# Wider projections and four query blocks at a time in a hybrid streaming-encoder block

## Chip and metric

The kernel runs on one core of one Trainium2 chip. The metric is device time in microseconds of one execution, median of several runs. Everything is single precision: operands are 32-bit, and a matrix product is done as three matmuls of split operands (below).

## The reference

One layer with 1024 tokens and 1024 channels. Three token mixers share one input projection; each is projected back to 1024 channels, gated and summed; then come an output projection, a residual and a gated feed-forward part. Shortened:

```python
h = rmsnorm(x, norm_mix_g); z = h @ w_in
hq, hf, hi, hg, fq, fk, fv, ff, mq, gate_logits = split(z)
y_a = hgrn2(hq, hf, hi, hg)            # 4 heads, 128x128 state
y_b = fox(fq, fk, fv, ff)              # 8 heads of 64
y_c = memory_attention(mq, mem_kv)     # 4 heads, 256 tokens
gates = sigmoid(gate_logits)           # 3 x 1024 columns
merged = sum(gates[b] * (y_b @ w_br[b]) for b in 3 branches)
x = x + merged @ w_out
x = x + (gelu(conv3(h2 @ w_up_a)) * (h2 @ w_up_v)) @ w_down   # 2816 wide
# fox, per head and block of 128 queries:
s = q @ k.T / 8 + F[q] - F[k]          # q, k normalised per head; k <= q
o = softmax(s) @ v
```

## The kernel before

A product is `mm3` (L158 to L162): both operands are split into a rounded high part and the rest, and three matmuls (high x high, high x low, low x high) accumulate in one PSUM bank. `split` (L172) casts on ScalarE and subtracts on VectorE. Weights come through `weights` (L188): a load from SP into one of two `raw` buffers, then a split into `wh` and `wl`, three buffers of each, 1024 columns a buffer.

The program is written as generators that are interleaved by `weave` and by priorities (`ahead`, a higher priority for the attention); the scheduler then puts the instructions of each engine into one fixed order, using a simulated timeline, before anything runs. `tc.issue_after(x)` puts an instruction behind `x` on the engine's queue. On the chip each engine works through its queue in order.

The stages, by the profile: the opening, the first gates and pairs of gate chunks as 7-product block multiplications (to about 200 us); values of the forgetting attention with the memory attention (to 310); the forgetting attention (to about 665); the recurrence with the branches' projections (to about 975); the output projection (to 1062); the way up (to 1477); the way down.

The forgetting attention is what most of the change touches. Heads come in four pairs `p`. `fox_proj(p)` (L844) projects the keys and queries of a pair, 256 columns, with `token_major` (L704): for each of 8 token blocks, 8 chunks x 3 matmuls with the tokens stationary and 256 columns moving. Its `evac` scales the result into `z` and, after four blocks, normalises it per head. `fox_prep(p)` (L866) transposes `z` and builds the split operands. `fox_attn(p, i)` (L901) takes the query blocks two at a time (`tp`): logits by two matmuls (L924, L925), masked maximum, exponential, reciprocal and scaling; then for each pair of key blocks transposes (L953 to L956) into one bank, a split, and products with the values (L965, L966) over 256 query columns; at the end of each of the four groups `yp` is added up and stored.

While a head runs, TensorE gets other work from the second argument of `weave`: for the first head of pair `p` the projection of pair `p + 1`, for the second head three gate chunks (`gates_early`, two halves of 24 matmuls of 512 columns each). During the last pair it is one gate and `hgrn_values` (L1012), the recurrence's values, in two parts of 256 columns.

Further on, `branch(br, ...)` (L1280) projects one branch: 8 chunks `j` x 2 halves, each step 12 matmuls of 512 columns, with the gates loaded back from memory from SP. Before `branch(0)` all eight loads of the memory branch's outcome (`yc`, 512 KB each) are issued from POOL. In the way up, `unit` (L1452) loads its weights in two halves from POOL into one of two `rw` buffers; `families` (L1495) makes the split block operands of the tokens, two of which (`B21`, chunks 2 and 3) have their subtraction on POOL.

Of the kernel before, what the change touches and what calls it, by code (L numbers as in the profile page):

```python
# [30 lines left out]
NFOX = [0, 3, 0, 3, 0, 3, 1]  # L31
# [3 lines left out]
assert 2 + NCOVER + NPAIR + sum(NFOX) == len(ORDER) and len(_dense) % 2 == 0  # L35
# [5 lines left out]
FOX_LATE = 0.2  # L41
SEQ = ("w0 x0 s0 w1 x1 s1 w2 x2 s2 w3 x3 s3 w4 x4 s4 x5 s5 x6 s6 x7 s7 u0 u1 u2 u3 mn u4 u5 u6 u7 lk k0 k1 k2 k3 lx "
# [67 lines left out]
def tile_block(ctx: ExitStack, tc: tile.TileContext, xT, memT, x_rows, mem_rows, vec, fbias, mats, hmask, w_first, w_cm, w_hi, w_fqk, w_fv,  # L110
# [77 lines left out]
    def weights(src, shape, raw=None, hl=None, parts=1):  # L188
# [4 lines left out]
        if hl is None:  # L193
            hl = [wp.tile([P, 4 * 264], F32R, tag=t, name=t, bufs=3) for t in ("wh", "wl")]
# [227 lines left out]
    def first_weights(k):  # L422
        k0, k1 = WFIRST[k]
        if k % 4 == 0:
            gw[k // 4] = [wp.tile([P, 4 * 264], F32R, tag=t, name=t, bufs=3) for t in ("wh", "wl")]
        sl = slice((k0 % 4) * 256, (k1 - 1) % 4 * 256 + 256)
        split(S, gw[k // 4][0][:, sl], gw[k // 4][1][:, sl], wg[k // 4][:, sl])
# [131 lines left out]
    class Dense:  # L559
# [16 lines left out]
        def operand(self, src):  # L576
            if self.half is None:
                self.half = [wp.tile([P, 4 * 264], F32R, tag=t, name=t, bufs=3) for t in ("wh", "wl")]
# [264 lines left out]

    def fox_proj(p):  # L844

        fox_z[p] = [None, None]

        def evac(tb, ps):
            n, b = tb // 4, tb % 4
            if b == 0:  # L850
                fox_z[p][n] = pq.tile([P, 4, 256], F32, tag="z", name=f"z{p}_{n}", bufs=2)
            z = fox_z[p][n]
            S.activation(z[:, b, :], ps, AF.Copy, scale=rt[:, tb:tb + 1])
            if b == 3:
                zz = z.rearrange("p b (h d) -> p (b h) d", d=64)
                sq = pools["pf"].tile([P, 16, 64], F32, tag="pt", name="fsq", bufs=4) if p else \
                    pm.tile([P, 16, 64], F32, tag="fsq", name="fsq")
                r = cp.tile([P, 16], F32, tag="fr", name="fr", bufs=2)
                S.activation(sq, zz, AF.Square)
                V.reduce_sum(r, sq, axis=AX.X)  # L860
                rstd_small(r, r, 64)
                V.tensor_mul(zz, zz, r.unsqueeze(2).to_broadcast([P, 16, 64]))

        yield from token_major(w_fqk[p], 256, evac)

# [35 lines left out]
    def fox_attn(p, i):  # L901
# [8 lines left out]
        for tp in range(4):  # L910
            pts = []
            for j in range(2):
                tb = 2 * tp + j
# [26 lines left out]
                S.activation(pt[:, :ns], pt[:, :ns], AF.Exp, bias=st[:, 2:3], accum_out=st[:, 3:4])  # L940
                V.reciprocal(st[:, 3:4], st[:, 3:4])  # L941
                G.tensor_scalar(pt[:, :ns], pt[:, :ns], st[:, 3:4], 0.0, ALU.mult, ALU.add)  # L942
# [3 lines left out]
            for sp in range(tp + 1):  # L946
                ptr = ps_tr()
                w = 384 if sp == tp else 512
                for jj in range(2):
                    sb = 2 * sp + jj  # L950
                    ssl = slice(sb * P, (sb + 1) * P)
                    if sb <= 2 * tp:
                        PE.transpose(ptr[:, jj * 256:jj * 256 + P], pts[0][:, ssl], ident)  # L953
                        PE.transpose(ptr[:, jj * 256 + P:jj * 256 + 256], pts[1][:, ssl], ident)
                    else:
                        PE.transpose(ptr[:, 256:384], pts[1][:, ssl], ident)  # L956
# [858 lines left out]
```

## Time and profile before

| | |
|---|---|
| median of 3 runs | 1699.96 us (1698.77 to 1700.16) |
| profiled execution, time | 1700.23 us |
| profiled execution, span from first to last instruction | 1698.4 us |
| mean granted TensorE clock | 0.999 |
| instructions | 24291, of which 8957 matmuls |
| moved by DMA | 227.16 MB, mean 134 GB/s |

The span is shorter than the time by what lies before the first and behind the last instruction. In the rows, PE is the matmul part of TensorE, PEld its loading of stationary operands (beside the matmuls), DVE VectorE, ACT ScalarE, POOL GpSimd, SP the engine that only issues DMAs. A group's row gives busy time and mean ns of one instruction, then the idle time just before them and what ended it. A timeline's row gives start, length, engine, line, operation, output and inputs, shape and count. A row of waits reads: who waited, for whom, total us, times, longest.

### The profile page before, as it was taken

The numbers are of one execution on the slowest core, as the hardware profiler recorded it, in microseconds if no ns is written. First come the engines' busy times: TensorE is split into PE (matmuls) and PEld (weight loads), VectorE is DVE, ScalarE is ACT, GpSimd is POOL, SyncE is SP. The second block draws the span as 40 slices with busy tenths as digits, with TensorE's granted clock in tenths as the row PEclk, the third lists the DMA queues.
The fourth block names the chain that finished last, engine by engine and source line by source line (L and its number), as shares of the span: only waits on it lengthen the run. The fifth ranks groups of instructions, "written<-read, shape, count | busy, mean of one in ns | idle before, by whom it ended". The sixth has DMA issues, their size and how long they took to land.

```text
span 1698.4 us, 24291 instructions
## 1 busy us (share of the span) xinstructions
PE 1691.0 (100%) x8957; PEld 1452.4 (86%) x8957; DVE 1150.8 (68%) x2057; ACT 800.9 (47%) x1428; POOL 324.6 (19%) x420
## 2 busy tenths in 40 slices
PE   9999999999999999999999999999999999999999
PEld 7888899989898998888888888888888888888887
DVE  6966455666666664886856845987878888775654
ACT  6734455545454553775631333644434444533432
POOL 0200032543433331544310000311111111100000
PEclk9999999999999999999999999999999999999999
DMA  9443232221212111110346542566544344494772
GB/s 367 157 161 106 88 139 68 77 92 51 94 59 77 63 46 57 67 32 13 106 127 209 167 186 100 165 174 169 158 139 138 118 149 143 172 363 145 251 269 87
DMA packets 83062, 227.16 MB, mean 134 GB/s; under 512 B 9712, under 2 KB 12408, under 8 KB 82816
## 3 DMA queue, kind: packets, MB, share of 16 engines
q1 hardware_dynamic: 64320, 160.54, 26.8%
q0 software_dynamic: 18048, 64.50, 13.2%
q8 instruction: 70, 1.15, 0.3%
q10 hardware_dynamic: 576, 0.59, 0.1%
q14 instruction: 48, 0.39, 0.1%
HBM read 180.72 MB, written 67.93 MB: 146 GB/s over the span
## 4 chain that ended last, share of the span: by engine, by line
PE 99%; DVE 0%; ACT 0%; DMA 0%; issue 0%; ACTq 0%; DVEq 0%
PE pp L160 21%; PE pp L162 21%; PE pp L161 21%; PE lg L160 4%; PE lg L162 4%; PE lg L161 4%; PE tr L162 3%; PE tr L161 3%; PE tr L160 3%; PE po L966 1%; PE lg L925 1%; PE lg L924 1%; PE po L965 1%; PE po L160 1%; PE po L161 1%; PE po L162 1%
## 5 line engine op out<-in xcount | busy, mean ns | idle before, releaser
L160 PE MATMUL pp<-uh,wh 128*128 128x512 f32 x412 | 163.3, 396 | 0.0
L161 PE MATMUL pp<-ul,wh 128*128 128x512 f32 x412 | 162.9, 395 | 0.0
L162 PE MATMUL pp<-uh,wl 128*128 128x512 f32 x412 | 162.5, 394 | 0.0
L161 PE MATMUL pp<-wl,uh 128*128 128x256 f32 (+1 forms) x512 | 146.3, 286 | 0.0
L162 PE MATMUL pp<-wh,ul 128*128 128x256 f32 (+1 forms) x512 | 146.1, 286 | 0.0
L160 PE MATMUL pp<-wh,uh 128*128 128x256 f32 (+1 forms) x512 | 145.6, 286 | 0.0
L166 ACT CAST wh<-s 128x512 fp32r<-128x512 f32 x110 | 66.5, 621 | 131.6 <-PE pp L161 55.1
L166 ACT CAST wh<-raw 128x1024 fp32r<-128x1024 f32 (+2 forms) x76 | 67.6, 890 | 100.6 <-PE pp L161 86.2
L166 ACT CAST wh<-rw 128x512 fp32r<-128x512 f32 x87 | 53.2, 619 | 108.1 <-PE pp L161 70.2
L160 PEld LDWEIGHTS pp<-wh,uh 128*128 128x128 f32 x512 | 97.3, 190 | 1.2
L161 PEld LDWEIGHTS pp<-wl,uh 128*128 128x128 f32 x512 | 97.4, 190 | 1.0
L162 PEld LDWEIGHTS pp<-wh,ul 128*128 128x128 f32 x512 | 97.4, 190 | 0.9
L1457 POOL DMA_DIRECT2D rw<-in_w_up x44 | 24.1, 555 | 372.4 <-DVE wl L1350 171.3
L166 ACT CAST dwh<-wr 128x1024 fp32r<-128x1024 f32 (+1 forms) x41 | 40.2, 980 | 115.8 <-PE tr L161 40.0
L162 PEld LDWEIGHTS pp<-uh,wl 128*128 128x128 f32 x412 | 77.5, 188 | 15.1
L174 DVE TENSOR_TENSOR wl<-raw,wh 128x1024 fp32r<-128x1024 f32 (+2 forms) x75 | 78.0, 1040 | 17.8 <-ACT wh L166 17.6
L160 PEld LDWEIGHTS pp<-uh,wh 128*128 128x128 f32 x412 | 77.5, 188 | 14.6
L161 PEld LDWEIGHTS pp<-ul,wh 128*128 128x128 f32 x412 | 77.5, 188 | 14.5
L940 ACT ACTIVATE pt<-pt,st 128x128 f32<-128x128 f32 (+3 forms) x64 | 49.7, 777 | 41.7 <-DVE st L937 33.9
L174 DVE TENSOR_TENSOR dwl<-wr,dwh 128x1024 fp32r<-128x1024 f32 (+1 forms) x41 | 46.3, 1129 | 31.7 <-ACT dwh L166 31.7
L942 POOL TENSOR_SCALAR pt<-pt,st 128x128 f32<-128x128 f32 (+3 forms) x64 | 49.1, 767 | 78.4 <-DVE st L941 64.1
L1350 DVE TENSOR_TENSOR wl<-rw,wh 128x512 fp32r<-128x512 f32 x69 | 47.7, 704 | 22.7 <-PE pp L162 18.2
(500 smaller groups left out, 5123.2 us busy)
## 6 DMA issues: line engine op xcount, KB each, us to landing
rw<-in_w_up POOLq DMA_DIRECT2D x44, 512.0 KB, 4.7
sd<-in_w_dn POOLq DMA_DIRECT2D x30, 512.0 KB, 6.0
br<-yd SPq DMA_DIRECT2D x30, 512.0 KB, 5.0
raw<-in_w_cm SPq DMA_DIRECT2D x24, 512.0 KB, 3.4
gd<-gt SPq DMA_DIRECT2D x48, 256.0 KB, 2.0
gt<-gd SPq DMA_DIRECT2D x48, 256.0 KB, 2.7
yd<-fc SPq DMA_DIRECT2D x44, 256.0 KB, 2.2
wr<-sd SPq DMA_DIRECT2D x20, 512.0 KB, 4.5
```

Of the source, the lines that this page charges most:

```text
L160: PE.matmul(ps, lh, rh, start=first, stop=False, skip_group_check=more)
L161: PE.matmul(ps, lh, rl, start=False, stop=False, skip_group_check=more)
L162: return PE.matmul(ps, ll, rh, start=False, stop=last, skip_group_check=more)
L166: return S.copy(out, in_)
L174: return (sub or V).tensor_sub(l, src, h.bitcast(F32))
L924: PE.matmul(ps[:, :w], qa[i][:, tsl], kh[i][:, s0:s0 + w], start=True, stop=False)
L925: fox_sets[p][3] = PE.matmul(ps[:, :w], qa[i][:, tsl], kl[i][:, s0:s0 + w], start=False, stop=True)
L940: S.activation(pt[:, :ns], pt[:, :ns], AF.Exp, bias=st[:, 2:3], accum_out=st[:, 3:4])
L942: G.tensor_scalar(pt[:, :ns], pt[:, :ns], st[:, 3:4], 0.0, ALU.mult, ALU.add)
L965: PE.matmul(o, vhl[:, sb, :], ph[:, src], start=(sb == 0), stop=False)
L1350: late["split"] = V.tensor_sub(l, src, h.bitcast(F32))
L1457: late["raw"] = G.dma_start(raw[:, 2 * i:2 * i + 2, :], src[:, 2 * i:2 * i + 2, :])
```

## The change

- Keys and queries of pairs 2 and 3 are projected together, 512 columns (`fox_proj_late`), each token block stored to memory (`zd`); `fox_load(p)` loads a pair back and normalises it. Pair 3's load runs in the second head of pair 1.
- The recurrence's values are projected in one part of 512 columns. `token_major` takes four weight buffers of two chunks for 512 columns, and `wh` and `wl` have four buffers (`WIDE`) instead of three.
- `fox_attn` takes four query blocks at a time: transposes of four blocks into one bank, products with the values over up to 512 columns, `yp` twice a head. `pt` has one buffer for each of the eight blocks.
- The norm's square goes through two halves in gate tiles (`fox_norm`).
- The ten early gates are spread differently over the heads (`first`, `second`).
- Each of the eight `yc` loads stands behind a one-column POOL operation that reads a gate tile just loaded, in steps 1, 2, 4, 5, 7, 8, 10 and 11 of `branch(0)`.
- The second unit's weight loads of the way up stand behind the last POOL subtraction of `B21`.
- The scratch of POOL's transfers is set to 4096 bytes.

```diff
-NFOX = [0, 3, 0, 3, 0, 3, 1]
+NFOX = 10
+WIDE = 4
@@ token_major
-            w = [weights(src[q], (4, ncol)) for q in range(2)]
+            per = 2 if ncol == HB else 4
+            w = [weights(src[q], (per, ncol)) for q in range(KC // per)]
...
-                wh, wl = w[k // 4]
-                mm3(ps, uh[k][:, tsl], ul[k][:, tsl], wh[:, k % 4, :], wl[:, k % 4, :], k == 0, k == KC - 1)
+                wh, wl = w[k // per]
+                mm3(ps, uh[k][:, tsl], ul[k][:, tsl], wh[:, k % per, :], wl[:, k % per, :], k == 0, k == KC - 1)
@@ before fox_proj
+    zd = tc.dram_tile([8, P, HB], F32, name="zd")
+    def fox_norm(z):
+        zz = z.rearrange("p b (h d) -> p (b h) d", d=64)
+        r = cp.tile([P, 16], F32, tag="fr", name="fr", bufs=2)
+        for i in range(2):
+            sq = gate_tile().rearrange("p (g d) -> p g d", d=64)
+            S.activation(sq, zz[:, 8 * i:8 * i + 8, :], AF.Square)
+            V.reduce_sum(r[:, 8 * i:8 * i + 8], sq, axis=AX.X)
+        rstd_small(r, r, 64)
+        V.tensor_mul(zz, zz, r.unsqueeze(2).to_broadcast([P, 16, 64]))
...
+    def fox_proj_late():
+        def evac(tb, ps):
+            t = gate_tile()
+            S.activation(t, ps, AF.Copy, scale=rt[:, tb:tb + 1])
+            SP.dma_start(zd[tb], t)
+        yield from token_major(w_late[0], HB, evac)
+    def fox_load(p):
+        cs = slice((p - 2) * 256, (p - 1) * 256)
+        for n in range(2):
+            z = fox_tile(p, n)
+            SP.dma_start(z, zd[4 * n:4 * n + 4, :, cs].rearrange("b p c -> p b c"))
+            fox_norm(z)
+            yield
@@ fox_attn
-        for tp in range(4):
+        for g in range(2):
...
-                pt = pf.tile([P, T], F32, tag="pt", name="pt", bufs=4)
+                pt = pf.tile([P, ns], F32, tag=f"pt{tb}", name=f"pt{tb}")
...
-            for sp in range(tp + 1):
+            for sb in range(4 * g + 4):
                 ptr = ps_tr()
+                first = max(sb - 4 * g, 0)
+                for j in range(first, 4):
+                    PE.transpose(ptr[:, j * P:(j + 1) * P], pts[j][:, sb * P:(sb + 1) * P], ident)
...
+                c = slice(first * P, HB)
+                split(S, ph[:, c], pl[:, c], ptr[:, c])
+                PE.matmul(po[:, c], vhl[:, sb, :], ph[:, c], start=sb == 0, stop=False)
+                PE.matmul(po[:, c], vhl[:, sb, :], pl[:, c], start=False, stop=sb == 4 * g + 3)
@@ the order of the pairs
+    late_proj = fox_proj_late()
+    first = (fox_proj(1), chain(islice(late_proj, 4), fox_load(2)), gates_early(2))
+    second = (chain(gates_early(1), islice(late_proj, 4)), gates_early(3), gates_early(3))
     for p in range(3):
-        weave((ahead(fox_attn(p, 0), AHEAD), FOX_STEPS), (fox_proj(p + 1), 8))
+        weave((ahead(fox_attn(p, 0), AHEAD), FOX_STEPS), (first[p], (8, 6, 4)[p]))
         fox_prep(p + 1, fox_sets[p][3])
-        weave((ahead(fox_attn(p, 1), AHEAD), FOX_STEPS), (gates_early(NFOX[2 * p + 1]), 2 * NFOX[2 * p + 1], FOX_LATE))
+        weave((ahead(fox_attn(p, 1), AHEAD), FOX_STEPS), (second[p], 6, FOX_LATE),
+              *([(fox_load(3), 2, 0.1)] if p == 1 else []))
+    run_all(late_proj)
@@ hgrn_values and the last pair
-        for pc in range(2):
-            def evac(tb, ps, pc=pc):
-                S.activation(Vf[:, tb, pc * 256:(pc + 1) * 256], ps, AF.Copy, scale=rt[:, tb:tb + 1])
-            yield from token_major(w_hi[pc], 256, evac)
+        def evac(tb, ps):
+            S.activation(Vf[:, tb, :], ps, AF.Copy, scale=rt[:, tb:tb + 1])
+        yield from token_major(w_late[1], HB, evac)
...
-        weave((ahead(fox_attn(3, i), AHEAD), FOX_STEPS), (islice(values, 8), 8),
-              (gates_early(0 if i else NFOX[6]), 2 * NFOX[6], FOX_LATE))
+        weave((ahead(fox_attn(3, i), AHEAD), FOX_STEPS), (chain(gates_early(1 - i), islice(values, 4)), 6 - 2 * i))
@@ loads of the memory branch
+            late["gates"] = gts[0]
...
+    first_branch = branch(0, yh, yl)
-    for c in range(4):
-        for t, d in zip(yc, ycd):
-            with tc.issue_after(state["norm"].ins):
-                G.dma_start(t[c], d[:, c, :].bitcast(F32R))
-    run_all(branch(0, yh, yl))
+    for i, _ in enumerate(first_branch):
+        if i % 3 and i < 12:
+            p, c = i % 3 - 1, i // 3
+            mark = G.tensor_scalar(warm, late["gates"][:, 0:1], 1.0, 0.0, ALU.mult, ALU.add)
+            with tc.issue_after(mark.ins):
+                G.dma_start(yc[p][c], ycd[p][:, c, :].bitcast(F32R))
@@ unit and families
-            late["raw"] = G.dma_start(raw[:, 2 * i:2 * i + 2, :], src[:, 2 * i:2 * i + 2, :])
+            with tc.issue_after(late["pool"].ins) if after else nullcontext():
+                late["raw"] = G.dma_start(raw[:, 2 * i:2 * i + 2, :], src[:, 2 * i:2 * i + 2, :])
...
-                    late["last"] = family_block(name, k, quarters(k)[q], G if name == "B21" and k > 1 else None)
+                    sub = G if name == "B21" and k > 1 else None
+                    late["pool" if sub else "last"] = family_block(name, k, quarters(k)[q], sub)
@@ kernel
-    nc = bacc.Bacc("TRN2", target_bir_lowering=False, num_devices=1)
+    nc = bacc.Bacc("TRN2", target_bir_lowering=False, num_devices=1, dynamic_dma_scratch_size=4096)
```

More of the change, by code (lines that the diff above doesn't have):

```diff
@@ L30 @@
 NDULL = 8
-NFOX = [0, 3, 0, 3, 0, 3, 1]
+NFOX = 10
 _dense = [12, 13, 14, 15] + [16 + 8 * br + j for br, j in ORDER[4:4 + NPAIR]]
 PAIRS = list(zip(_dense[0::2], _dense[1::2]))
-assert 2 + NCOVER + NPAIR + sum(NFOX) == len(ORDER) and len(_dense) % 2 == 0
+assert 2 + NCOVER + NPAIR + NFOX == len(ORDER) and len(_dense) % 2 == 0
 FOX_STEPS, HGRN_STEPS, MEM_STEPS = 28, 14, 7
@@ L193, in weights @@
         if hl is None:
-            hl = [wp.tile([P, 4 * 264], F32R, tag=t, name=t, bufs=3) for t in ("wh", "wl")]
+            hl = [wp.tile([P, 4 * 264], F32R, tag=t, name=t, bufs=WIDE) for t in ("wh", "wl")]
         for i in range(parts):
@@ L577, in operand @@
             if self.half is None:
-                self.half = [wp.tile([P, 4 * 264], F32R, tag=t, name=t, bufs=3) for t in ("wh", "wl")]
+                self.half = [wp.tile([P, 4 * 264], F32R, tag=t, name=t, bufs=WIDE) for t in ("wh", "wl")]
                 h, l = (t[:, :HB] for t in self.half)
@@ L1776, in pieces @@
         return out
-    o["w_hi"] = c(np.stack(pieces(hi, [(0, 256), (256, 512)])))
     o["w_fqk"] = c(np.stack([pieces(np.concatenate([fk[:, p * P:(p + 1) * P], fq[:, p * P:(p + 1) * P]], axis=1),
-                                    [(0, 256)])[0] for p in range(4)]))
+                                    [(0, 256)])[0] for p in range(2)]))
+    late = np.concatenate([m[:, p * P:(p + 1) * P] for p in (2, 3) for m in (fk, fq)], axis=1)
+    o["w_late"] = c(np.stack([kmaj(m).reshape(P, 4, 2 * HB).transpose(1, 0, 2) for m in (late, hi)]))
     pv = pieces(np.concatenate([fv, ff], axis=1), [(0, 256), (256, 520)])
```

57 lines of the change are left out of this document (17 added, 40 removed).

## The prediction

> **What bounds the kernel now.** I read the page's head and engine rows first, then TensorE's waits, then the busy time by stretch, then single instructions.
>
> ```profile
> span 1698.4 us, 24291 instructions
> ...
> PE 1691.0 (100%) x8957; PEld 1452.4 (86%) x8957; DVE 1150.8 (68%) x2057; ACT 800.9 (47%) x1428; POOL 324.6 (19%) x420
> ```
> ```profile
> PE lg L160 <- ACT uh L349: 1.8, 1, 1.8
> PE tr L265 <- POOL dull L263: 1.0, 1, 1.0
> PE po L1189 <- DVE St L1195: 0.7, 1, 0.7
> PE pp L162 <- DVE wl L1350: 0.2, 1, 0.2
> ```
> ```profile
> 310.00:700.00 390.00, 390.00 (x2561) 355.68 (x2560) 242.82 (x686) 204.72 (x400) 141.93 (x184) 1.00 0.21 69
> 885.00:930.00 45.00, 45.00 (x202) 37.02 (x201) 29.71 (x43) 8.79 (x15) 4.52 (x9) 1.00 0.70 231
> 1065.00:1085.00 20.00, 19.82 (x103) 16.53 (x103) 18.09 (x32) 14.24 (x27) 9.78 (x10) 1.00 0.46 159
> 0.00:10.00 10.00, 7.17 (x26) 6.04 (x27) 4.46 (x12) 5.36 (x10) 0.44 (x6) 0.87 0.82 284
> ```
>
> TensorE is the bound. It is busy for 1691.0 of 1698.4 us, and its recorded waits are 3.7 us in all, 2.8 of them in the opening that the change leaves alone. In the columns of the second fence (length, then PE, PEld, DVE, ACT, POOL) the stretch of the forgetting attention, 310 to 700 us, has TensorE busy for all of its 390 us, VectorE for 243 and ScalarE for 205. So work taken from VectorE, ScalarE or the DMA queues is worth nothing there, and there is almost no wait to remove (0.9 us after the opening). Only cheaper TensorE work can shorten the kernel, and a new TensorE wait lengthens it by its full size. Because matmuls overlap, the price of one is the distance from its start to the next start, not its recorded length.
>
> **What the change does to TensorE's own work.** First, 256-column projections become 512-column ones.
>
> ```profile
> L160 PE MATMUL pp<-wh,uh 128*128 128x256 f32 x448 | 127.1, 285 | 0.0
> ```
> ```profile
> 331.58 0.28 PE L161 MATMUL pp<-wl,uh 128*128 128x256 f32 x1
> ...
> 333.73 0.28 PE L161 MATMUL pp<-wl,uh 128*128 128x256 f32 x1
> ```
> ```profile
> 349.26 0.39 PE L160 MATMUL pp<-uh,wh 128*128 128x512 f32 x1
> ...
> 352.67 0.39 PE L160 MATMUL pp<-uh,wh 128*128 128x512 f32 x1
> ...
> 354.48 0.40 PE L160 MATMUL pp<-uh,wh 128*128 128x512 f32 x1
> 354.71 0.40 PE L161 MATMUL pp<-ul,wh 128*128 128x512 f32 x1
> 354.95 0.39 PE L162 MATMUL pp<-uh,wl 128*128 128x512 f32 x1
> ...
> 355.87 0.39 PE L160 MATMUL pp<-uh,wh 128*128 128x512 f32 x1
> ```
>
> Between 331.58 and 333.73 lie 18 starts of 256 columns: 0.1194 us each. Between 349.26 and 352.67 lie 15 of 512 columns: 0.2273 each; between 354.48 and 355.87, right behind attention steps, six: 0.2317 each. I take 0.2295, the middle, since both kinds of place occur. A wide instruction instead of two narrow ones saves 2 x 0.1194 - 0.2295 = 0.0093 us, by the two ends 0.0115 and 0.0071. There are 3 x 448 = 1344 such narrow instructions. Pairs 2 and 3 of the attention (2 sets x 8 blocks x 8 chunks x 3 = 384) and the recurrence's values (another 384) become 384 wide ones: 384 x 0.0093 = 3.6 us saved (4.4 and 2.7 by the ends). The values of attention and pairs 0 and 1 stay.
>
> The Trainium skill (TensorE: Matmul & The Clock Gate, "Wait — 56ns, not 53.3ns?") puts the fixed cost of a warm matmul at about 2.5 ns on top of its columns; by that alone the pair would save 2.5 ns, and 384 of them an estimated 1.0 us. The rows above show four times as much, so the trace does not agree, and the sum goes by the rows.
>
> Second, the product with the values (L965, L966) over four query blocks.
>
> ```profile
> L966 PE MATMUL po<-pl,vhl 128*128 128x256 f32 x128 | 34.7, 293 | 0.0
> L966 PE MATMUL po<-pl,vhl 128*128 128x128 f32 x32 | 8.9, 278 | 0.0
> ```
> ```profile
> 339.12 0.22 PE L965 MATMUL po<-ph,vhl 128*128 128x128 f32 x1
> 339.18 0.28 PE L966 MATMUL po<-pl,vhl 128*128 128x128 f32 x1
> 339.29 0.30 PE L953 MATMUL tr<-ident,pt 128*128 128x128 f32 x1
> ```
>
> L965 has the same counts. Per head that is now 32 instructions of 256 columns and 8 of 128; a 128-column one takes 0.06, or 0.11 where a transpose follows: 32 x 0.1194 + 4 x 0.06 + 4 x 0.11 = 4.50 us. Afterwards it is 12 of 512, 4 of 384 (estimate 0.1745, midway between 256 and 512), 4 of 256 and 4 of 128: 2.75 + 0.70 + 0.48 + 0.34 = 4.27 us. Columns are the same, 9216. Saved: 0.23 x 8 heads = 1.8 us (1.6 to 2.1 by the two wide prices). The transposes stay 36 per head, but in 12 groups instead of 10, so there are 16 more switches between matmul and transpose; the row at 339.18 shows 0.05 for one, so the bill lies between 0 and 0.8. I take 0.4. TensorE's own work falls by 3.6 + 1.8 - 0.4 = 5.0 us.
>
> **What lies beside it.** The split weights are the same 12 halves of 1024 columns for these projections; evacuation is half as many ScalarE instructions of twice the width; the square and sum in the norm become two halves each; splits of the transposed probabilities are two more per head but no more columns, and the evacuation of the outcome half as many. All of this is on ScalarE and VectorE, idle for 185 and 147 us of the 390: nothing. Cover for TensorE per head hardly moves: a half projection is 96 wide instructions, 22.0 us, where 192 narrow ones took 22.9.
>
> The late pairs now go out to memory (8 stores) and come back (4 loads) through SP, then through the norm:
>
> ```profile
> rw<-in_w_up POOLq DMA_DIRECT2D x44, 512.0 KB, 4.7
> ...
> gd<-gt SPq DMA_DIRECT2D x48, 256.0 KB, 2.0
> ...
> mqf<-mqd SPq DMA_DIRECT2D x4, 512.0 KB, 4.2
> ...
> ycl<-ycld POOLq DMA_DIRECT2D x4, 512.0 KB, 9.6
> ```
> ```profile
> L166 ACT CAST wh<-raw 128x1024 fp32r<-128x1024 f32 x26 | 27.2, 1045 | 21.7 <-PE pp L161 18.3 <-PE pp L162 3.3
> ...
> L859 ACT ACTIVATE fsq<-z 128x1024 f32<-128x1024 f32 x7 | 7.4, 1062 | 2.4 <-PE tr L953 2.4
> ```
> ```profile
> L174 DVE TENSOR_TENSOR wl<-raw,wh 128x1024 fp32r<-128x1024 f32 x26 | 32.0, 1230 | 12.6 <-ACT wh L166 12.6
> ...
> L862 DVE TENSOR_TENSOR z<-z,fr 128x1024 f32<-128x1024 f32 x7 | 10.3, 1469 | 0.7 <-POOL fr L179 0.7
> ...
> L860 DVE TENSOR_REDUCE fr<-fsq 128x16 f32<-128x1024 f32 x7 | 8.5, 1216 | 1.3 <-ACT fsq L859 1.3
> ```
> ```profile
> L179 POOL TENSOR_TENSOR fr<-fr,mhalf 128x16 f32<-128x16 f32 x7 | 20.7, 2962 | 13.7 <-DVE fr L178 10.7 <-DVE st L941 2.8
> ```
> ```profile
> SPq L185 <- DVE wl L174: 156.7, 39, 20.0
> ```
>
> If ScalarE's and VectorE's slack were gone, the 16 more splits would cost at most half of the 1.05 us of a 1024-column cast each, 8 us. From the last late block to a usable pair 2: store 2.0, reload 4.2, square 1.06, sum 1.22, power 2.96, scaling 1.47: 12.9 us. Its user is fox_prep(2), behind which stands a head with three gates, 144 x 0.2295 = 33 us of TensorE work: I cost it at 0. Pair 3, moved ahead by a head, has more room still. Behind a reload that waits on SP stand the stores of gates and outcomes, the next head's bias row and the next weights; SP already waits up to 20 us at a time (last row) with no TensorE wait to show for it. The late projection holds all four weight buffers, so the next unit's weights wait for its last block. They then need 1.05 + 1.23 = 2.3 us, and the block still has 18 x 0.2295 = 4.1 us to run from where the first buffer is free: 0, or up to 2 us at each of the two ends if the splits queue.
>
> The memory branch's eight loads are tied to the first branch's gate loads, each behind a one-column POOL operation. In 885 to 930 POOL is busy for 4.5 of 45 us and TensorE for all of it, so nothing is there to win. The last load hangs on step 11 of 16, and four steps of 12 x 0.2273 are 10.9 us against a landing of 9.6: 0, with 1 or 2 us at risk.
>
> The way up's second load now goes behind the POOL split:
>
> ```profile
> 1068.02 1.05 POOL L1457 DMA_DIRECT2D rw<-in_w_up  x2 [13.69 <-ACT B22h L166]
> ...
> 1075.13 2.98 POOL L174 TENSOR_TENSOR B21l<-x,B21h 128x512 fp32r<-128x512 f32 x2 [0.23 <-ACT B21h L166]
> ```
> ```profile
> 1082.36 0.39 PE L162 MATMUL tr<-B21h,wl 128*128 128x512 f32 x1
> 1082.93 0.50 PE L162 MATMUL pp<-B11h,wl 128*128 128x512 f32 x1 [0.18 <-DVE wl L1350]
> ```
>
> The load could not start before 1078.1 and would land at about 1082.8, with cast and subtraction still to come, where TensorE wants its first operand at 1082.9. This stretch is tight (VectorE busy 18.1 of 20 us). Against it, the first unit's last product, 12 x 0.2273 = 2.7 us, can be put ahead. Bounds: -0.2 (today's wait gone) to +2.0; I take +0.5, nearer to the cover. The smaller scratch for POOL's transfers shows in no row here; no TensorE wait names a POOL transfer, so I take 0, with the 2 us of the other bounds as its risk.
>
> **The sum.** -5.0 + 0.5 = -4.5 us. The profiled execution took 1700.23 us, 0.27 above the median shown: 1695.7 against itself, 1695.5 on the median's footing. About 0.2%, 3.4 us, is what a measurement of this kernel can tell from no change.
>
> **Rivals.** *Slower: the order on TensorE puts the reloaded pair's transposes too early.* TensorE takes its queue in the written order. If fox_prep's transposes of pair 2 or 3 stand directly behind the last late block, the 12.9 us are exposed: +8.4 net, 1708.4. It makes the kernel slower beyond measurement once 7.9 us are exposed, and eats the gain to within it from 1.1 us on. For it: the present kernel has no such round trip to memory in this stage. Against it: 33 us of cover, and zero waits in 390 us today. The opening shows what waiting does to the granted clock, 0.87 over the first 10 us. The Trainium skill (the same page, Part 1) says one idle window of about 3.4 us halves the clock; by it a stall of that size would cost an estimated 1.7 us more.
>
> *No change: wide is no cheaper in the mix.* The start at 354.71 is followed at 354.95, 0.24 us, as much as two narrow ones. If all wide ones next to attention work went so, the projections would save nothing (-0.5) and the products 0.10 a head, 0.8: 1699.7. The long run at 0.2273 speaks against it. By the skill's 2.5 ns the outcome lies here too, an estimated 1.3 us saved for 512 instructions fewer; the rows bear neither out.
>
> *Same: several small waits.* Weights late at both ends, the way up at its bound: 2 + 2 + 1.5 beyond my sum, 1701.0. Decides once over 1.1 us are exposed.
>
> **How the numbers follow.** Forecast 0.60 (1693.0 to 1696.5); small waits 0.12, wide no cheaper 0.06; the reload's order 0.22, mostly with part of the 12.9 us. Faster 0.60, same 0.19, slower 0.21. Low is the sum by the good ends, 4.4 + 2.1 + 0.2 = 6.7: 1693.3, so 1693.0. High, 1703.5, takes in the small waits and the lesser reload stalls, and leaves out about 0.18.
>
> **What would show it.** TensorE matmuls 8957 - 384 - 128 = 8445, the group of 256-column matmuls of L160 down from 448 to 192, wide starts near 0.23 us, and TensorE's waits after the opening under 2 us. Wrong would be a wait at fox_prep's transposes (L878 now), at the first matmul of a gate behind the late blocks, or at the second unit of the way up, or wide starts at 0.24.

## The result and the profile after

| | before | after |
|---|---|---|
| median | 1700.06 us (1698.77 to 1700.18) | 1720.84 us (1719.82 to 1722.57) |
| profiled execution, time | 1700.23 us | 1719.89 us |
| span | 1698.4 us | 1717.9 us |
| mean granted TensorE clock | 0.999 | 0.995 |

After to before is 1.0125, 95% interval 1.0107 to 1.0143: 20.8 us slower, where 4.5 us faster was forecast and 1703.5 was the upper end. One execution of the kernel before and one of e15, both near 2833 us, and one of e10 at 9159 us (runs described below) are left out of the ratios. The page's head, engine rows and one group of the changed kernel:

```profile
span 1717.9 us, 23220 instructions
...
PE 1696.8 (99%) x8445; PEld 1429.4 (83%) x8445; DVE 1154.9 (67%) x2065; ACT 794.9 (46%) x1420; POOL 324.8 (19%) x428
```
```profile
L161 PE MATMUL pp<-wh,uh 128*128 128x256 f32 x192 | 55.0, 286 | 0.0
```

The work changed as foreseen: 8445 matmuls, 192 narrow ones left of 448 a line. TensorE still looks busy, but 21.1 us of the span are now idle instead of 7.4, and busy time holds slow matmuls too. Its waits in the changed kernel:

```profile
PE lg L949 <- DVE qa L916: 4.0, 1, 4.0
PE pp L161 <- DVE gt L1065: 2.8, 1, 2.8
PE tr L162 <- DVE B21l L175: 1.8, 1, 1.8
PE lg L949 <- DVE st L955: 1.7, 2, 0.9
```

These rows name 10.3 us, and all rows after the opening together 14. The rest shows only in the stretches (length, PE, PEld, DVE, ACT, POOL with counts, granted clock, DMA share, GB/s):

```profile
413.00:440.00 27.00, 27.00 (x137) 22.66 (x137) 19.26 (x37) 13.60 (x23) 10.95 (x7) 1.00 0.39 133
440.00:455.00 15.00, 13.14 (x61) 9.87 (x60) 11.40 (x48) 8.60 (x20) 6.32 (x11) 0.77 0.17 54
455.00:467.00 12.00, 7.94 (x49) 6.53 (x48) 11.84 (x43) 9.39 (x20) 7.01 (x12) 0.99 0.26 69
...
600.00:612.00 12.00, 10.71 (x61) 8.12 (x60) 10.23 (x38) 7.88 (x17) 2.77 (x5) 1.00 0.00 1
688.00:699.00 11.00, 8.23 (x31) 6.37 (x30) 7.37 (x12) 7.16 (x10) 6.16 (x4) 0.84 0.38 116
1084.00:1102.00 18.00, 14.13 (x59) 10.04 (x58) 14.47 (x24) 10.08 (x19) 8.47 (x11) 0.91 0.43 150
```

Below, *excess* is what the distances from one matmul's start to the next add up to in a stretch beyond the usual distance of their kinds, so it counts idle time and half-clock matmuls alike. Before the change, outside the opening, it is 0.9 us. After it is 10.7 at 442 to 470 us (first head of pair 1), 2.0 at 601 to 611, 4.5 at 691 to 698, 6.2 at 1084 to 1101 (way up): 23.4 us. Less 4 to 5 us of cheaper TensorE work (below) that is 18 to 19 of the 19.5 us between the spans. The size of one place in one trace is good to about 3 us only: e7 and e13 (below) run the same instructions in the same order as the changed kernel on every engine up to 1083 us, and yet e7 has 14.0 us at the first place where the changed kernel and e13 have 10.7, and both have about 3 at 691 where the changed kernel has 4.5.

The first place, read back from its effect. The `mm3` high x high product (L161, one of the three matmuls in all spare work) and the attention's logits (L950) in stretches; then ScalarE, POOL, SP's reloads and VectorE there (start, length):

```profile
417.00:440.00 23.00, 9.85 (x26) 4.70 (x25) 1.00 0.42 142
440.00:467.00 27.00, 0.06 (x1) 0.09 (x1) 0.87 0.21 60
467.00:490.00 23.00, 11.41 (x27) 5.37 (x27) 0.93 0.36 128
```
```profile
417.00:440.00 23.00, 0.67 (x2) 0.56 (x3) 1.00 0.42 142
440.00:467.00 27.00, 6.39 (x18) 3.45 (x18) 0.87 0.21 60
```
```profile
426.72 1.15 ACT L853 ACTIVATE gt<-z 128x512 f32<-128x512 f32 x2 [2.34 <-DMA z<-zd]
430.59 0.97 ACT L167 CAST ph<-tr 128x512 fp32r<-128x512 f32 x2 [2.71 <-PE tr L975]
...
465.59 1.13 ACT L853 ACTIVATE gt<-z 128x512 f32<-128x512 f32 x2
```
```profile
428.97 2.90 POOL L180 TENSOR_TENSOR fr<-fr,mhalf 128x16 f32<-128x16 f32 x1 [2.74 <-DVE fr L179]
431.84 0.46 POOL L944 TENSOR_TENSOR nfm<-nf,mskf 128x128 f32<-128x128 f32 x1
```
```profile
422.38 0.38 SPq L888 DMA_DIRECT2D z<-zd  x1
...
461.41 0.38 SPq L888 DMA_DIRECT2D z<-zd  x1
```
```profile
466.16 0.69 DVE L465 TENSOR_TENSOR gt<-pp,rx 128x512 f32<-128x512 f32 x1
```

Pair 2's norm runs at 420 to 433 us. On ScalarE its squares wait for the reload (2.34 us) in front of the attention's splits, on POOL its second power (428.97) stands in front of the attention's mask (431.84), and the attention gets on slowly: 2 logits of this line in 23 us. The same stretch has 3 in e4 and in e8 (both with this reload of pair 2) and 7 in e5 (no reload), whose row is:

```profile
417.00:440.00 23.00, 2.54 (x7) 1.32 (x7) 1.00 0.25 84
```

So the reload thins out the attention here. Which step of the norm does it is not shown: the split behind the squares (430.59) waits another 2.71 us for TensorE's transposes, which stand behind gates in TensorE's own order. TensorE does not idle meanwhile: from 418.0 to 439.8 it runs the next spare work, 72 matmuls of gates, three halves of 24, each into a PSUM bank of its own. They are not emptied: the gate's evacuation (466.16) comes behind pair 3's norm (465.59), whose load (461.41) waits for `fox_prep`'s transposes of pair 2 (460.2 to 461.3) to free a `z` buffer. So from 440 to 467 us TensorE has 1 spare product of line L161 where the stretches beside it have 26 and 27; it runs the attention alone, at the speed of its chain (VectorE is busy for 11.84 of the 12 us from 455), and falls to half clock.

### The profile page after: what moved, and what is told of

It is laid out like the page before. It is cut to its first block, busy times and chain, and to the rows that moved or that the text cites. A ratio compares the mean times of both kernels' runs of the same rounds, so it can differ in the third digit from the quotient of the medians.

```text
span 1717.9 us, 23220 instructions
## 1 busy us (share of the span) xinstructions
PE 1696.8 (99%) x8445; PEld 1429.4 (83%) x8445; DVE 1154.9 (67%) x2065; ACT 794.9 (46%) x1420; POOL 324.8 (19%) x428
## 3 DMA queue, kind: packets, MB, share of 16 engines
q0 software_dynamic: 18048, 64.50, 13.1%
## 4 chain that ended last, share of the span: by engine, by line
PE 86%; issue 9%; DVE 2%; DMA 1%; ACT 1%; POOL 0%; ACTq 0%; POOLq 0%; DVEq 0%
PE pp L161 18%; PE pp L162 18%; PE pp L163 18%; PE lg L161 4%; PE lg L163 4%; PE lg L162 4%; PE tr L161 3%; PE tr L162 3%; PE tr L163 3%; PE tr L975 2%; PE po L161 1%; PE po L981 1%; PE po L163 1%; PE po L162 1%; PE po L980 1%
## 5 line engine op out<-in xcount | busy, mean ns | idle before, releaser
L161 PE MATMUL pp<-uh,wh 128*128 128x512 f32 x412 | 165.1, 401 | 2.8 <-DVE gt L1065 2.8
L162 PE MATMUL pp<-wl,uh 128*128 128x256 f32 (+2 forms) x384 | 123.7, 322 | 0.0
L161 PE MATMUL pp<-wh,uh 128*128 128x256 f32 (+2 forms) x384 | 123.6, 322 | 0.1
L163 PE MATMUL pp<-wh,ul 128*128 128x256 f32 (+2 forms) x384 | 123.4, 321 | 0.0
L161 PEld LDWEIGHTS pp<-uh,wh 128*128 128x128 f32 x412 | 78.2, 190 | 18.3 <-DVE gt L1065 3.2
L167 ACT CAST ph<-tr 128x512 fp32r<-128x512 f32 (+1 forms) x96 | 43.2, 479 | 83.6 <-PE tr L975 78.9
L161 PEld LDWEIGHTS pp<-wh,uh 128*128 128x128 f32 x384 | 72.8, 190 | 5.2 <-ACT Vf L1034 0.2
L163 PEld LDWEIGHTS pp<-wh,ul 128*128 128x128 f32 x384 | 72.8, 190 | 5.1
L162 PEld LDWEIGHTS pp<-wl,uh 128*128 128x128 f32 x384 | 72.8, 190 | 4.9
L175 DVE TENSOR_TENSOR pl<-tr,ph 128x512 fp32r<-128x512 f32 (+1 forms) x96 | 50.9, 550 | 29.8 <-ACT ph L167 28.8
L955 DVE CUSTOM_DVE_ANT_0 pt<-lg,nf 128x512 f32<-128x512 f32 (+2 forms) x80 | 41.0, 524 | 38.6 <-PE lg L950 20.1
```

The lines of the kernel that those rows point to most:

```text
L161: PE.matmul(ps, lh, rh, start=first, stop=False, skip_group_check=more)
L162: PE.matmul(ps, lh, rl, start=False, stop=False, skip_group_check=more)
L163: return PE.matmul(ps, ll, rh, start=False, stop=last, skip_group_check=more)
L167: return S.copy(out, in_)
L175: return (sub or V).tensor_sub(l, src, h.bitcast(F32))
L955: V.tensor_tensor_reduce(out=pt[:, s0 + lo:s0 + hi], in0=ps[:, lo:hi], in1=bias, op0=ALU.add, op1=ALU.max, scale=1.0, scalar=-3e38, accum_ ...
```

## The experiments

The kernel before, measured beside each run, has medians of 1699.8 to 1700.2 us. Differences between runs are differences of medians.

| run | what it is | median, us | ratio, 95% interval | excess after the opening, by place |
|---|---|---|---|---|
| e1 | before + 4 weight buffers | 1705.35 | 1.0022 to 1.0050 | way up 6.6 |
| e15 | e1 + power behind first load | 1702.45 | 1.0006 to 1.0025 | way up 3.5 |
| e2 | before + four query blocks | 1717.15 | 1.0089 to 1.0121 | 611: 1.8; 681 to 714: 7.6; 909 to 923: 11.6 |
| e14 | e15 + wide values | 1708.66 | 1.0043 to 1.0069 | 586 to 605: 6.3; 714: 1.3; way up 4.2 |
| e18 | reload alone | 1711.40 | 1.0053 to 1.0083 | 447 to 467: 10.8; way up 2.7 |
| e3 | after, two query blocks | 1718.14 | 1.0090 to 1.0126 | 446 to 470: 12.1; 608: 2.0; way up 5.6 |
| e4 | after, pair 3 back a head later | 1718.31 | 1.0095 to 1.0127 | 488 to 498: 6.8; 590 to 604: 6.6; 610: 1.8; way up 6.9 |
| e5 | after, no way through memory | 1709.68 | 1.0047 to 1.0077 | 588 to 604: 5.5; way up 6.6 |
| e6 | after, narrow values | 1715.85 | 1.0080 to 1.0113 | 442 to 470: 10.7; way up 6.9 |
| e7 | after, power behind first load | 1717.96 | 1.0096 to 1.0126 | 442 to 473: 14.0; 611: 2.0; 693: 2.9; way up 4.4 |
| e8 | after, squares in own buffer | 1718.63 | 1.0098 to 1.0128 | 580 to 612: 16.3; way up 6.6 |
| e9 | after, loads not spread | 1718.63 | 1.0099 to 1.0129 | as after |
| e13 | after, way up repaired | 1715.13 | 1.0078 to 1.0110 | way up 2.6; 691: about 3; the rest as after |
| e10 | after, nothing wide | 1713.40 | 1.0062 to 1.0096 | 680 to 702: 9.1; way up 6.1 |
| e11 | e10, 3 weight buffers | 1719.80 | 1.0103 to 1.0133 | 612: 1.8; 681 to 703: 9.4; 911 to 923: 8.7; way up 3.5 |
| e12 | e6, pair 2 in place | 1727.69 | 1.0153 to 1.0187 | 488 to 506: 12.3; 625: 1.9; 694 to 716: 8.7; way up 7.0 |
| e16 | e14 + third `vhl` buffer | 1715.87 | 1.0075 to 1.0109 | 672 to 708: 12.2; way up 4.1 |
| e17 | e16 + second load ahead of power | 1714.19 | 1.0067 to 1.0097 | 673 to 709: 12.7; way up 2.6 |

None beats the kernel before.

**The way up: e1, e7, e13, e15, e11.** In e1 the kernel before gets `bufs=4` for `wh`, `wl` and `sums`, and the scratch of 4096 bytes that makes room.

> The kernel before with nothing changed but four weight buffers instead of three and the smaller scratch. Theory A (the way up is late because with four buffers the first load of the way up is written behind the power of the second norm on POOL's queue): +4 to +7 us, all of it between the last product of the output projection and the second unit, and no new wait in the attention. Theory B (the hold of the second load causes it, or the thinner attention): within 1 us of the kernel before.

POOL's queue at the second norm in the changed kernel, in e1, before, and in e15:

```profile
1083.45 2.03 POOL L180 TENSOR_TENSOR rt<-rt,mhalf 128x8 f32<-128x8 f32 x1 [149.59 <-DVE rt L179]
1085.45 1.12 POOL L1479 DMA_DIRECT2D rw<-in_w_up  x2
```
```profile
1070.63 2.04 POOL L179 TENSOR_TENSOR rt<-rt,mhalf 128x8 f32<-128x8 f32 x1 [180.83 <-DVE rt L178]
1072.64 2.15 POOL L1457 DMA_DIRECT2D rw<-in_w_up  x4
```
```profile
1053.27 1.06 POOL L1457 DMA_DIRECT2D rw<-in_w_up  x2 [163.03 <-ACT sqs L1392]
...
1071.70 2.65 POOL L179 TENSOR_TENSOR rt<-rt,mhalf 128x8 f32<-128x8 f32 x1 [2.63 <-DVE rt L178]
```
```profile
1069.39 2.04 POOL L1508 TENSOR_TENSOR rt<-rt,mhalf 128x8 f32<-128x8 f32 x1 [27.62 <-DVE rt L1417]
1071.39 1.11 POOL L1457 DMA_DIRECT2D rw<-in_w_up  x2
```

With four buffers the power stands ahead of the way up's first loads, and they are issued 19 us later in e1 than before, 32 us in the changed kernel, which is only some 12 us behind by then. So a fourth buffer comes with another written order here and costs 5.4 us, all at the way up, as the first expectation had it. e7 puts the power back behind the load:

```diff
-        rstd_small(rt2, ps[:, :8], D)
+        V.tensor_scalar(rt2, ps[:, :8], 1.0 / D, EPS, ALU.mult, ALU.add)
...
+                with tc.issue_after(late["raw"].ins):
+                    G.tensor_tensor(rt2, rt2, mhalf[:, :8], ALU.pow)
```

> The changed kernel with one order changed: on POOL the power of the second norm stands behind the first load of the way up. If that order is the cause of the way up's late start: the waits between 1084 and 1101 us (6.2 us over the plain rate, half of it the halved clock) go, 1713 to 1716 us. If the held second load is the cause, they stay: 1719 to 1722.

The time fell by 2.9 us, to between the two expectations, and of the way up's 6.2 only 1.8 came back. e13 also drops the hold of the second load, e15 does e7's edit on e1:

> The changed kernel with the hold of the way up's second load taken off and the second norm's power put behind the first load on POOL, so that POOL's queue stands there as before the change. If the two are separate causes of the same standstill (the power first with four buffers: 6.6 us in the run of four buffers alone; the hold: 3.5 us in the run of three buffers), the cluster at 1084 to 1101 us goes from 6.2 to under 1.5 us and the time to 1714.5 to 1716.5 us. If four buffers make the way up slow by something else than POOL's order, 4 us or more stay there and the time is 1717 or more.

> The kernel before with four weight buffers and the power behind the way up's first load, nothing else. If the 5.4 us of four buffers alone were only POOL's order there, they go: 1699 to 1701 us, with no cluster of excess over 1.5 us from 1065 to 1100. If not, 1703 or more. Its difference to the run before it is the price or gain of the wide values by themselves.

e13 gained 5.7 us on the changed kernel, as expected in the time, though 2.6 us stay at the way up. By e7 and e13 the power's place is worth 2.9 us and the hold another 2.8; each step's interval overlaps with the next. e15 gained 2.9 on e1 and did not reach 1701, so the power's place is about half of the fourth buffer's cost: the last fence shows the second unit's loads now behind the power, where they stood ahead of it before (1068.02). What the last 2.6 us are is open; e17, where that load is ahead too, still has them.

**The way through memory: e5, e18, e3, e4, e12.** e5 projects pairs 2 and 3 in place with 256 columns; three gates go to each second head, as before.

> The changed kernel with pairs 2 and 3 projected as before, 256 columns in place, without the way through memory; gates 3, 3, 3, 1 as before; four blocks, wide values, four weight buffers, way up as changed. If the late projection's way through memory is behind the long stall of pair 1 (excess 11 us in 440 to 470): that stall goes; about 2.5 us of narrower matmuls come back; 1708 to 1712 us. If four blocks do it: the stall stays near the end of pair 1 and the time is above 1716.

11.2 us come back and the place at 440 is gone, for 2.5 us of cheaper projections given up. e18 is the converse: two query blocks, narrow values, loads not spread, the way up in e17's order, and the reload.

> The way through memory by itself: two query blocks, narrow values, four weight buffers and a way up in the order of the run before it; pairs 2 and 3 projected together, stored and loaded back as in the changed kernel. If the reload alone brings the standstill, the cluster at 440 to 470 us is there with 10 to 12 us (as in the run with two blocks) and the time is 1706 to 1711. If it needs wide values or four blocks beside it, there is under 3 us of excess and the time is 1697 to 1700.

```profile
417.00:444.00 27.00, 11.35 (x29) 5.45 (x29) 1.00 0.41 135
444.00:468.00 24.00, 1.40 (x2) 0.66 (x2) 0.86 0.19 59
468.00:490.00 22.00, 10.56 (x27) 5.08 (x27) 1.00 0.30 107
```

The same hole in line L161 as in the changed kernel, without wide values or four blocks: the reload makes it with only what comes with it (its order of the gates, squares in gate tiles, four weight buffers). e3 has two blocks beside everything else, and the hole too (12.1 us):

> The changed kernel with the attention of two blocks put back; everything else as changed. Theory A (projections and reload): still 12 us or more slower than before, with the long wait about 440 to 470 us. Theory B (four blocks): the waits in the attention go and 5 us or less are left, those of the way up.

e4 loads pair 3 back in the first head of pair 2 (`chain(fox_load(3), gates_early(2))`), so that no norm stands before the gate's evacuation:

> The changed kernel with pair 3's reload back in the first head of pair 2. Theory A (the gates of pair 1's second head wait for gate tiles that are reserved for pair 3's norm, whose load waits for pair 2's transposes; three PSUM banks fill and TensorE runs out of work): the stall about 440 to 466 us goes, 8 to 14 us less than the changed kernel, unless pair 3 is then late for its own head. Rival (the norm of pair 2 holds up the attention on POOL's queue by itself): the stall stays, within 3 us of the changed kernel.

The place is empty, as the expectation's theory A had it, but the time is only 2.5 us lower: 6.8 us stand at 488 to 498, where pair 3 now returns, and 6.6 at 590. e12, with narrow values, writes pair 2's half straight into `z`, stores only pair 3's and loads it back where e4 does:

```diff
+            S.activation(z[:, b, :], ps[:, :256], AF.Copy, scale=rt[:, tb:tb + 1])
...
-            S.activation(t, ps, AF.Copy, scale=rt[:, tb:tb + 1])
-            SP.dma_start(zd[tb], t)
+            S.activation(t[:, :256], ps[:, 256:], AF.Copy, scale=rt[:, tb:tb + 1])
+            SP.dma_start(zd[tb, :, 256:], t[:, :256])
```

> The changed kernel with narrow values, and with the late projection still 512 columns wide, but pair 2's half evacuated straight into its tiles and normalised there; only pair 3's half goes through memory and comes back in the first head of pair 2. If the standstill at 440 to 470 us comes from the reloaded pair's norm and loads standing in the queues, half of the reload gives back most of it and keeps the 2.5 us of cheaper projection: 1705 to 1710 us. If any pair that comes back through memory makes it, the standstill moves behind pair 3's load (480 to 510 us, as when that load was moved alone) with 6 us or more, and the time is 1712 to 1717.

Worse than both expectations: 12.3 us behind the one reload, with 13.7 us of half clock, and a bare end at 694. Half the round trip is not half the stall.

**What takes one blocker away moves the stall: e8, e6, e14, e16, e17.** e8 gives the squares two own buffers (scratch 2048 bytes), so that the norm holds no gate tile:

> The changed kernel with the norm's squares in a buffer of their own instead of gate tiles (and a scratch of 2048 bytes to make room). If gates stand behind gate tiles that the reloaded pair's norm has reserved: gates can be emptied during pair 1's second head, and the stall of 442 to 470 us goes or falls below 3 us, 1707 to 1714 us. If the reload holds the attention up by its norm's place on the in-order queues alone: within 3 us of the changed kernel.

The hole at 440 is gone, so it takes the gate tiles that the norm holds; but the time is within 2.2 us of the changed kernel's, because this stands in its place (L161, 579 to 612 us), not one spare product in 33 us:

```profile
440.00:467.00 27.00, 10.56 (x27) 5.07 (x27) 1.00 0.32 101
...
579.00:612.00 33.00, 0.00 (x0) 0.00 (x0) 0.84 0.08 25
```

e6 has the recurrence's values in two parts of 256 columns again:

> The changed kernel with the recurrence's values in two parts of 256 columns again. If wide values fill three banks that cannot be emptied before the last heads' values are split: the waits about 600 to 611 us go (2 us and part of what follows), 2.5 us of wider matmuls are lost, 1718 to 1721 us. If not, the waits stay at that place.

5.0 us better, more than its two expectations had it: the waits at 601 to 611 and the 4.5 us at 691 both went. e14 is the wide values by themselves on e15, with `chain(gates_early(0 if i else 1), islice(values, 4))` in the last pair's heads:

> The kernel before with only the recurrence's values projected 512 columns wide (two query blocks, pairs in place, loads as before), the four weight buffers that this needs, and the power put behind the way up's first load. If wide values save their 2.5 us (192 pairs at 0.0131 us) where two blocks keep the attention's end short and the order on POOL is as before, 1697 to 1699 us: faster than both kernels. If the wide blocks fill the banks because they wait for all 512 columns of their target, whatever the attention's blocks, 2 to 5 us of excess stay between 575 and 700 us and the time is 1700 to 1704.

6.2 us slower than e15 although 192 pairs of matmuls became cheaper. The evacuations into `Vf` before and in e14 (durations, then first and last start), and e14's spare work (L160):

```profile
L1015 ACT ACTIVATE Vf<-pp,rt x16: 454/474/482, 554.6 to 639.1; 128x256 f32<-128x256 f32 x16
```
```profile
L1015 ACT ACTIVATE Vf<-pp,rt x8: 681/687/693, 605.6 to 646.5; 128x512 f32<-128x512 f32 x8
```
```profile
586.00:606.00 20.00, 0.00 (x0) 0.00 (x0) 0.91 0.12 37
```

A narrow block can go into columns that old values have left; a wide one needs all 512, and the last of them are read by the split of head 7's values (603.7 to 605.6 us in e14), which waits for a `vhl` buffer that head 5 holds. The wide blocks wait in the banks, and the attention runs bare until 605.6. e16 adds the buffer (`bufs=3`), e17 also issues the second unit's loads before the power:

> The kernel of wide values alone, with a third buffer for the split values of a head (vhl; the room comes from a scratch of 2048 bytes). The split of head 7's values need not wait for head 5's last product any more. If the cluster of 6.3 us at 586 to 605 us comes from wide blocks that hold the PSUM banks until that split has read the old values, it goes, and the time falls from 1708.7 to 1701 to 1703 us (the way up's 4 us stay). If the gates and wide blocks running ahead make it whatever the buffer, it stays or moves, with over 1707.

> The same with the second unit's loads of the way up put ahead of the power on POOL as well. The 3.5 to 4.2 us left at the way up in the last two kernels are put down to those loads standing 3.4 us later behind the power. If that is so, the cluster goes and the time is 1697 to 1699 us, 2.5 us below the kernel before for the cheaper projection. If something else makes it, the time stays within 1 us of the run before it.

e16's first evacuation is at 571.9, and the place is clean (20 products of L160 from 586 to 606 us), so the cause of e14's stall there is shown. It is nonetheless 7.2 us slower than e14. Its spare work (L160) in the last head, and that stretch before the change:

```profile
672.00:696.00 24.00, 2.46 (x5) 1.33 (x5) 0.86 0.16 51
```
```profile
672.00:690.00 18.00, 8.72 (x24) 4.32 (x23) 1.00 0.31 103
```

The spare work that no longer stood still was used up early; the last head then had 5 products of this line in 24 us, where the kernel before has 24 in 18. As I read it, the blocked columns had been keeping cover back for the end. e17's way up has 2.6 us instead of 4.1, but its time fits neither expectation: 1.7 us below e16's, with overlapping intervals.

**Four query blocks and the spread loads: e2, e9, e10, e11.** e2 puts the new `fox_attn` into the kernel before (squares in gate tiles, scratch 4096).

> The kernel before with only the attention over four blocks (and the norm's square in gate tiles, the smaller scratch, three weight buffers). Theory A (the waits come from the projections and the reload, the four blocks by themselves are a small gain): 1 to 3 us faster than before, TensorE waits under 1 us between 310 and 700 us. Theory B (the longer chain of four softmaxes starves TensorE): 5 to 15 us slower, with waits at the transposes.

Neither place was right. The attention has 1.8 us to 680, then a bare end (7.6), and the largest loss is in the first branch: a TensorE wait, SP's queue ahead of it, and where SP does the same before the change:

```profile
PE pp L160 <- DVE gt L1282: 9.1, 1, 9.1
```
```profile
898.07 7.53 SPq L1325 DMA_DIRECT2D x<-in_xT  x8
...
907.86 0.33 SPq L1275 DMA_DIRECT2D gt<-gd  x1
```
```profile
977.18 3.99 SPq L1336 DMA_DIRECT2D x<-in_xT  x8
```

Eight loads of 512 KB for the residual have come 79 us earlier in SP's written order, ahead of a gate's load, which then takes 9.8 us to land. I first took it for the collision of the `yc` loads; e9 (changed kernel, eight loads together again) says no:

> The changed kernel with the eight loads of the memory branch issued together again before the first branch, as before the change. If the attention over four blocks alone creates the wait of 9 us behind a gate's load near 909 us (seen in the run of the four blocks alone), and the spreading is its repair, that wait comes back here: a TensorE wait of 8 to 10 us on gt between 890 and 930 us and 9 to 14 us more than the changed kernel, 1730 to 1735 us. If that wait belonged to the order of that one kernel, there is none here and the time stays within 2 us of the changed kernel's 1720.8.

No wait at 909; the time is 2.2 us below the changed kernel's, with overlapping intervals. The spread is worth nothing measurable here. e10 undoes both wide projections, e11 has three buffers (`WIDE = 3`) as well:

> The changed kernel with both wide projections undone: pairs 2 and 3 projected in place with 256 columns, and the recurrence's values in two parts of 256. Four blocks, four weight buffers, spread loads and the held load stay. If the excess of each part is its own (no way through memory was worth 11.2, narrow values 5.0), the two add up: 1704 to 1707 us, with excess left only at the way up (about 6 us). If the attention only moves its standstill to the next full set of banks, as when pair 3's reload was moved, 5 us of excess stay between 570 and 690 us and the time is 1709 to 1712.

> The kernel of the run before with three weight buffers in place of four: what is left of the change is four query blocks, the squares in gate tiles, the spread loads, the held load of the way up and the smaller scratch. If four buffers cost the way up its 5.4 us whatever else is there, this is 5 to 6 us below the run before and level with the unchanged kernel: 1699 to 1702 us, and no cluster of excess over 2 us near 1070 to 1100. If the held load itself keeps the way up waiting, the excess there stays at 3 us or more and the time above 1703.

e10 misses its sum (1720.8 less 11.2 and 5.0) by 8.7 us, and lies 1.4 us above its second expectation too: with nothing wide the bare end at 680 to 702 appears, which e5 and e6 don't have. In e11 the fourth buffer's cost at the way up fell as meant (6.1 to 3.5, the hold remaining), but the residual's loads again stand before a gate's (900.48 on SP, spread or not), 8.7 us. So that wait comes with four blocks and three buffers, in e2 and e11, and with four buffers nowhere. Why the written order flips there is open.

## Why the prediction was wrong

**TensorE as the bound: right,** and so was the warning that a new wait costs its full size. Its sum for TensorE's own work, -5.0 us, holds to about 1 us, but with one term too small and one too large. *Projections:* from 310 to 700 us a narrow matmul takes 0.1226 us from start to start on average before, a wide one 0.2321 after: 0.0131 a pair, 5.0 us for 384, where 0.0093 and 3.6 stood. The clean run of 0.1194 that I took for narrow ones was too good. *Products with the values:* products and transposes together, from start to start, take 62.4 us before and 61 to 63 in e2 once its waits are taken out (66.0 with them), so of the 1.4 net of switches 1 us at most was there. "Wide no cheaper" falls (and its 1699.7 left out the switches and the way up, 0.9 us of the forecast's own terms), and the Trainium skill's 2.5 ns for the fixed cost of a matmul (TensorE: Matmul & The Clock Gate, "Wait — 56ns, not 53.3ns?") is too small against these 13.1 ns a pair.

**What failed is the step "I cost it at 0" for what lies beside TensorE,** above all the reload. Its chain was sized about right: 12.9 us stood there, and from the last store (420.17) to the scaled pair (433.38) it took 13.2. The gates that were to cover it were there too; but I took cover as something that lies in wait until needed. Here the gates ran while the chain did: the attention got on slowly beside it, 72 matmuls of gates were done by 440, and their results then stood in full banks until pair 3's reload was in (466.16). e5 and e18 show 11 us for the reload. "Pair 3 has more room still" failed with it: its early load is what held the banks (e4), and put later it made a stall of its own.

**Wide values** were costed as a saving only; e14 against e15 shows +6.2, and e6 gives back 5.0. I looked at instruction counts and not at what the target's columns wait for. **Weight buffers:** the bound was 2 us at two ends of the projection, the cost 5.4 us at the way up (e1), a stage where I gave them nothing. **The way up:** forecast +0.5 with +2.0 as its end; the cluster is 6.2, of which e13 takes away 3.6 (its time is 5.7 us lower). The cause looked for (the late second load) was half of what the two edits give back. **Spread loads at 0:** right (e9). **Four blocks** were given a TensorE saving and no tail: alone they cost 17 us (e2), from a bare end and a changed order on SP.

**The rival "slower"** had the sign and the reload as its source, and the wrong place: not `fox_prep`'s transposes wait (the largest named wait there is that of the next pair's logits for `qa`, 4.0 us, which `fox_prep` makes) but the attention itself runs uncovered. "Several small waits" at 1701.0 had one place right, the way up, at a third of its size. The warning on the clock came true (below).

The parts do not add up: against the kernel before, four buffers are 5.4 us, wide values 6.2 on top of e15, the reload with four buffers 11.2, four blocks with three buffers 17.2, and the whole 20.8. As I read it, what they share is one stock of cover, and each moves the place where it runs out; no run here counts that stock by itself.

## What to carry to other kernels

Where an engine is kept full by spare work, count not only how much there is but when each piece can start and what lets its PSUM bank go: spare work runs ahead during any hold-up, and if its evacuation waits on the held-up chain, the stall comes afterwards and elsewhere. Taking one blocker away can only move such a stall; compare the filler's own instructions stretch by stretch, since waits named in the profile showed 14 of 23 us. And after an edit to buffers, compare the order on the DMA-issuing queues in stages that the edit doesn't touch: there the fourth weight buffer cost 5.4 us and the residual's early loads a wait of 9.1.

## What the hardware showed

The granted clock halves in steps of 3.4 us, also when TensorE was not idle. The changed kernel around the first place:

```profile
442.80:446.20 3.40, 2.14 (x10) 1.28 (x9) 3.40 (x12) 1.80 (x4) 0.00 (x0) 0.99 0.02 5
446.20:453.00 6.80, 6.20 (x23) 4.74 (x23) 4.48 (x22) 3.56 (x9) 3.67 (x6) 0.50 0.37 116
453.00:463.20 10.20, 9.22 (x56) 7.38 (x54) 9.40 (x40) 7.65 (x19) 6.48 (x12) 1.00 0.04 12
463.20:466.60 3.40, 0.32 (x3) 0.35 (x4) 3.34 (x12) 3.35 (x6) 2.13 (x3) 1.00 0.57 173
466.60:470.00 3.40, 3.40 (x10) 2.72 (x10) 3.27 (x8) 1.44 (x3) 2.05 (x3) 0.51 0.75 214
```

Behind a step with TensorE busy for 2.14 of 3.40 us, a share of 0.63 (busy as the profile has it, with modelled ends), the clock is at 0.50 for two steps; behind one with 0.32 of 3.40 us it is so for one. Cut into these steps, the traces of all the kernels here agree after the opening: a full-clock step with a share below 0.45 is always followed by half clock, one above 0.63 never. In between both happen: 0.47 in the changed kernel (1094.7 to 1098.1 us) is followed by half clock, 0.46 in e3 (1091.8 to 1095.2) is not. What decides there, no run here separates. The Trainium skill (TensorE: Matmul & The Clock Gate, Part 1) has the half clock follow an idle window of about 3.4 us: step and size agree, but the window need not be idle, as the share of 0.63 shows. The changed kernel runs 17 us at half clock in four places behind its stalls, e5 none outside the opening and the end.
